# A two-layer hybrid decoder trunk on one core: direct key and value products in layer 0, its first gate's dots beside them, sums of squares by tokens in the opening, attention's turns counted from zero

## The chip, the core and the metric

The kernel runs on one core of a Trainium2 chip. The core has a matrix engine (TensorE; PE in the profile, its weight loads PEld), a vector engine (VectorE, DVE), a scalar engine (ScalarE, ACT), GpSimd (POOL) and SyncE (SP), which here only issues DMAs. The metric is the device time of one execution in microseconds, lower is better. All arithmetic is in float32; matrix products are made of float32 operands that are split in two parts, `hi` (in the format `fp32r`) and `lo` (the remainder), with three matmuls for each product: hi x hi, hi x lo and lo x hi.

## The reference, cut to what matters

Two layers over 512 tokens of 1024 channels. What the change touches is the first norm, the keys and values, and the gate `g1`:

```python
def hybrid_layer(x, c_act, ...):
    mod = (c_act @ w_ada + b_ada)[:, None, :]
    sh1, sc1, g1, sh2, sc2, g2 = jnp.split(mod, 6, axis=-1)
    h = rmsnorm(x, norm1_w) * (1 + sc1) + sh1
    u = h @ w_in
    u_pool, u_conv, b_conv, c_conv, q, k, v, gate_logits = jnp.split(u, offsets, axis=-1)
    y_pool = pool_mixer(u_pool, pool_w, pool_scale)
    y_conv = b_conv * causal_short_conv(c_conv * u_conv, conv_w)
    q = apply_partial_rope(rmsnorm(q.reshape(B, S, ATTN_HEADS, HEAD_DIM), q_norm_w), cos, sin)
    k = apply_partial_rope(rmsnorm(k.reshape(B, S, ATTN_HEADS, HEAD_DIM), k_norm_w), cos, sin)
    o = moba_attention(q, k, v)
    gates = jax.nn.sigmoid(gate_logits).reshape(B, S, N_BRANCH, D)
    merged = gates[:, :, 0] * (y_pool @ p_pool) + gates[:, :, 1] * (y_conv @ p_conv) + gates[:, :, 2] * (y_attn @ p_attn)
    x = x + g1 * (merged @ w_out)
    h2 = rmsnorm(x, norm2_w) * (1 + sc2) + sh2
    return x + g2 * ((jax.nn.silu(h2 @ w_gate) * (h2 @ w_up)) @ w_down)
```

`mod` has six parts of 1024 numbers (SH1, SC1, G1, SH2, SC2, G2 in the kernel). Each is a product of one vector with a 1024 x 1024 matrix.

## The kernel before

Activations are kept with channels on the 128 partitions and 512 tokens along the free axis, as 8 tiles. A product with a weight column is one "feature tile": 8 steps over the channels, `mm3` (L163) each, three matmuls of 512 columns.

**The stream of weights.** `items` (L374 to L389) lists the weight tiles (128 x 1024, 512 KB) in the order of use. `next_w` (L454) hands out the next one and loads up to four ahead (`load_w`, L433). A load takes one of three buffers of the ring `raw`; `split_w` (L397) then makes `hi` on ACT (L399) and `lo` on DVE (L402), each with five buffers. Some columns are split by transfer instead (`split_by_transfer`, L416): ACT makes `hi` and its negative, and a DMA of POOL's queue adds the weight to it in memory (L423). The loads are issued by SP, in order.

**Dots.** Each of the 6 x 8 pieces of `mod` of a layer is one instruction on DVE: `ada_dot` (L477, recorded as L479) multiplies a 128 x 1024 tile of `w_ada` with the conditioning vector and sums. `ada_tasks` (L530) makes a list of them with a cost of 1.2 each. With `early`, tiles come from the ring `raw`, loaded one dot ahead; without, from the pool `w4`.

**Turns.** Every `mm3` counts its columns in `clock[0]`. At 2048 columns (four products of 512) `tick` (L139) is called: it advances the fibers (attention, written as generators, which yield the number of turns to wait) and runs tasks of the queue `bulk`, as far as a credit goes that grows by `bulk_rate` for each turn, up to 4. PE's and DVE's main instructions are kept in the order of the program (`keep_in_program_order`, `pin`).

**Opening.** PE first runs idle matmuls (`WARM`, `WARM2`). x is squared on DVE and ACT (L894, L899), added in pairs on DVE (L901), and four fp32 matmuls with a matrix of ones (L902) leave the sum of squares of each token, on all partitions, as 128 x 512 numbers. ACT takes the inverse root (L908) and its scaled square (L909), two wide steps on DVE (L913, L914) refine it into `norm.rstd`, and `first_scaled` (L657) multiplies x with it. Two dots, SC1 and SH1 of tile 0, stand ahead of the refinement on DVE. Then `first_hi` (L661) makes the first operand of PE. After that, for every channel tile: two dots, scale, split of the weights, `lo`.

**Keys and values.** `keys_values` (L1001) computes the 1024 columns of keys and values with seven products of half-size blocks in place of eight (rows of tokens in two halves, channels in two halves; the names B21, B11, R1, -V, B22, T3, T4 are the forms). `sums_one` and `sums_two` (L986, L996) make the sums of activations on DVE; the class `KeyValue` (L296) loads the weights and lets DMAs of POOL's queue, DVE (L338) and `split_rows` make the sums of weights. Keys and queries are squared, normalised and rotated (`turn`, tasks of `bulk`), and values are split into `v`.

**Attention and gates.** The fiber `attention` (L858) starts five turns after the values. PE meanwhile computes gates (`gate`, L1176, tanh on ACT in L1180), convolution, and pooling branch (two products of 512 columns with `pw`, L1198). `gated` (L1209) multiplies a gate with its branch. In layer 0 the SC2 dots run here (L1202). Then come the attention branch (GATE2, L1232): a gate, a product, two steps on DVE and a split (`split_from`, L675 and L676). In this loop layer 0 runs the dots of G1 and SH2 (rate 1.5), layer 1 those of G1 (rate 1.3). The loop `tail` (L1261) makes the output projection with the residual, which needs `g1` and `merged`.

**After.** Second norm, feed-forward (also by seven products, `glu_pair`), and the next layer.

Of the kernel before, what the change touches and what calls it, by code (L numbers as in the profile page):

```python
# [73 lines left out]

WARM = 9

WARM2 = 19

GATE2 = ([("gate", j) for j in range(6)] + [("attn", 0), ("attn", 1), ("gate", 6), ("gate", 7)]
         + [("attn", j) for j in range(2, 8)])  # L80
# [3 lines left out]
def hybrid_trunk(ctx, tc, xT, ws, ada, cols, pool_w, qk_w, crow, pos, con, out):  # L84
# [69 lines left out]
    def matmul(*a, **k):  # L154
        tc.keep_in_program_order(T.matmul(*a, **k))  # L155
# [140 lines left out]
    class KeyValue:  # L296
# [25 lines left out]
        def load(self, sub):  # L322
            form, cp = divmod(sub, 2)
            if sub == 0:
                self.near, self.far = [None] * 2, [None] * 2
            if sub == 2:
                self.x = [w4([P, C_BLOCKS, P]) for _ in range(2)]
                for i in range(2):
                    self.summed(self.x[i], (1, 1), i)
            if form < 2:  # L330
                kk = 1 - form
                raw = self.raw(kk, 0, cp)
                if form == 1:
                    self.near[cp] = raw
                return split_by_transfer(raw, self.l, self.blocks(kk, 0, cp)) if self.l == 0 else split_w(raw, C_BLOCKS)
            if form in (2, 3):
                w = split_w(self.x[cp], C_BLOCKS)
                pin(V.tensor_add(self.x[cp], self.x[cp], self.near[cp]))  # L338
                if form == 2:
                    self.near[cp] = self.raw(1, 0, cp)  # L340
                    self.far[cp] = [bigt(F32) for _ in range(2)]
                    self.summed_rows(self.far[cp], (0, 0), cp)
                return w
            if form == 4:
                return split_w(self.x[cp], C_BLOCKS)
            if form == 5:
                return split_rows(self.far[cp])
            return split_w(self.raw(1, 1, cp), C_BLOCKS)
# [26 lines left out]
    for l in range(L):  # L375
        first_part = [b for b in _plan() if b[0][0] not in ("gate", "up", "down")]
        keys = [b for b in first_part if b[0][0] == "in" and KEYS <= b[0][2] < KEYS + 8]
        at_keys = first_part.index(keys[0])
        column_of = {b[0][2]: b for b in first_part if len(b) == KT and b[0][0] == "in"}
        moved = [column_of[n] for n in AFTER_KEYS]  # L380
        first_part = [b for b in first_part if b not in keys and b not in moved]
        first_part[at_keys:at_keys] = [KeyValue(l)] + moved
        for blocks in first_part + list(feed_forward()):
            if not isinstance(blocks, list):
                if isinstance(blocks, int):
                    blocks = GateUp(l, blocks)
                items += [(blocks, sub) for sub in range(blocks.SUBS)]
            else:
                items.append((None, (l, blocks)))  # L389
# [189 lines left out]


    class Norm:
        def __init__(self, one=False):
            self.one = one
            self.low = []
            self.acc = bigt(F32)
            self.last = bigt(F32)
            self.sums = [(bigt(), bigt()) for _ in range(1 if one else 2)]
            self.rstd = bigt(F32)
            self.hi = [bigt() for _ in range(KT)]
            self.lo = [bigt() for _ in range(KT)]  # L590
            self.h = [bigt(F32) for _ in range(KT)]
# [278 lines left out]


    scratch = ps_pair()
    norm = Norm()

    rows = [ps_mm(), ps_mm()]
    for i in range(WARM):
# [4 lines left out]
        if i == 6:  # L881
            for j in range(KT):
# [6 lines left out]
    pin(V.scalar_tensor_tensor(abias, colt[:, 0, C_ADA + SC1 * KT:C_ADA + (SC1 + 1) * KT], 1.0,  # L889
                               minus, op0=ALU.add, op1=ALU.mult))  # L890
    sq = [bigt(F32) for _ in range(KT)]
    for k in range(KT):
        if k == 0 or (k % 2 == 1 and k < KT - 1):
            step.append(pin(V.tensor_mul(sq[k], x[k], x[k])))  # L894
        else:
            if k in (2, 4):
                h = k // 2 - 1
                pin(A.activation(csil[:, h * S:(h + 1) * S], rows[h], AF.Copy))
            pin(A.activation(sq[k], x[k], AF.Square))  # L899
        if k % 2 == 1:  # L900
            step.append(pin(V.tensor_add(sq[k], sq[k - 1], sq[k])))  # L901
            matmul(scratch[:, 0], ones, sq[k], start=(k == 1), stop=(k == KT - 1))  # L902
    first[0].update(ada_first_load(0, step[3], (SH1,)))
    idle = ps_mm()
    for _ in range(WARM2):
        matmul(idle[:, :P], ones, ones, start=True, stop=True)
    y, y2, t = bigt(F32), bigt(F32), bigt(F32)
    A.activation(y, scratch[:, 0], AF.Abs_reciprocal_sqrt, bias=epst, scale=1.0 / D)  # L908
    split_after[0] = A.activation(y2, y, AF.Square, scale=(0.5 / D) ** 0.5)  # L909
    ada_first(0, first[0], SC1)  # L910
    ada_first(0, first[0], SH1)

    pin(V.scalar_tensor_tensor(t, scratch[:, 0], D * EPS, y2, op0=ALU.add, op1=ALU.mult))  # L913
    pin(V.scalar_tensor_tensor(norm.rstd, t, 1.5, y, op0=ALU.subtract, op1=ALU.mult))  # L914
    norm.first_scaled(0)
    norm.first_hi(0)
    fetch_after[0] = step[4]
# [19 lines left out]
    for l in range(L):  # L937
# [63 lines left out]
        def keys_values(qk, ss, made, tables, then):  # L1001
# [60 lines left out]
                V.tensor_add(part[t], part[t], d[t])  # L1062
            yield from enumerate(part)

        pw = {}

        def pool_weights():
# [58 lines left out]
        for j in range(2):  # L1126
            if j == 1:
                pu = ps_mm()
                feature_tile(pu, next_w())
                made = [sums_one(0), sums_one(1)]  # L1130
                uc[1] = bigt(F32)
                A.activation(uc[1], pu, AF.Copy)
            pc = ps_mm()
            feature_tile(pc, next_w())
            flush_bulk()
            if j == 1:
                made += [sums_one(2), sums_one(3)]
            z = bigt(F32)
            V.tensor_mul(z, pc, uc[j])
            zs.append(z)  # L1140
# [23 lines left out]
            bulk_rate[0] = 1.4  # L1164

        bulk_rate[0], credit[0] = 0.0, -1.0
        v = [[bigt().rearrange("p (n h d) -> p n h d", n=4, h=2) for _ in range(TT)] for _ in range(2)]
        for t, src in keys_values(qk, ss, made, tables, turn):
            for half in range(2):
                part = src[:, half * BLOCK:(half + 1) * BLOCK].rearrange("p (n d) -> p n d", d=HD)  # L1170
                o = v[half][t]
                A.activation(o[:, :, 0], part, AF.Copy, scale=-1.0)
                V.scalar_tensor_tensor(o[:, :, 1], part, -1.0, f32(o)[:, :, 0], op0=ALU.mult, op1=ALU.subtract)
        flush_bulk()
# [6 lines left out]
            return sg  # L1181

        m01, y_attn = [], []
        fibers.append([5, attention(l, qk, v, nrq, prq, y_attn)])
        bulk.append((0.4, pool_weights))
        for j in range(2):
# [45 lines left out]
        for step, j in GATE2:  # L1232
# [3 lines left out]
            if j == 0:  # L1236
                drain()
                flush_bulk()
                if l == 0:
                    bulk.extend(ada_tasks(l, (SH2,)))  # L1240
                late = len(bulk)
                bulk.extendleft(reversed(ada_tasks(l, (G1,))))
                bulk_rate[0] = 1.5 if l == 0 else 1.3
            if j % 2 == 0:
                aw_ = next_w()
            p1 = ps_mm()
# [324 lines left out]
```

## Time and profile before

| what | value |
|---|---|
| runs, device us | 1446.49, 1443.2, 1445.98 (median 1445.98) |
| profiled execution, from its first to its last instruction | 1440.7 us, granted clock 0.999 |
| opening, up to 16.2 us | PE busy 14.1 us, DVE 11.0, DMA share 0.90 |
| first products of layer 0, 16.2 to 71.7 | PE 55.3 of 55.5 us, DVE 48.6 |
| keys and values of layer 0, 71.7 to 110.6 | PE 38.5 of 38.9 us, DVE 36.8, ACT 29.8 |
| gates and attention of layer 0, 110.6 to 299.6 | PE 186.8 of 189.0 us, DVE 135.1 |
| attention branch of layer 0 and what follows, 299.6 to 345.0 | PE 42.9 of 45.4 us, DVE 43.4, granted clock 0.96 |
| gates and attention of layer 1, 823.8 to 1011.3 | PE 185.8 of 187.5 us, DVE 125.7 |
| attention branch of layer 1, 1011.3 to 1050.0 | PE 38.7 of 38.7 us, DVE 32.8 |

The last seven rows are from the view that gives each engine's busy time in stretches of the span. The span is what the profiler saw of one execution; the runs are 2.5 to 5.8 us longer. Matmuls are pipelined and overlap in the records, so PE's busy time hides small gaps: the starts of successive matmuls tell more.

### The profile page before, as it was taken

How to read it: one execution, taken by the hardware profiler on the slowest of the kernel's cores; microseconds unless marked ns; L12 is line 12 of the kernel's file. 1: busy time of each engine (PE TensorE's matmuls, PEld its weight loads, DVE VectorE, ACT ScalarE, POOL GpSimd, SP SyncE). 2: the span in 40 equal slices, each digit the busy share in tenths (PEclk: the TensorE clock that was granted, in tenths of full speed). 3: DMA queues.
4: the chain of work that ended last, by engine and by line, in shares of the span. 5: the costliest groups of instructions: out<-in, count | busy, mean ns of one | idle time of the engine just before them, and what ended most of it. 6: DMA issues, size and time to landing. Idle time of an engine off the chain costs nothing.

```text
span 1440.7 us, 22089 instructions
## 1 busy us (share of the span) xinstructions
PE 1428.3 (99%) x8298; PEld 1253.2 (87%) x8298; DVE 1062.3 (74%) x1944; ACT 750.8 (52%) x1260; POOL 165.7 (12%) x230
## 2 busy tenths in 40 slices
PE   9999999999999999999999999999999999999999
PEld 7887788887989998989988887888889989989997
DVE  8899767579786867767789986665878747657663
ACT  6776666633554452535454675666336525525450
POOL 0111000101100210211002000011020102111200
PEclk9999999999999999999999999999999999999999
DMA  9877666697446766747528665567773537646532
GB/s 359 234 199 192 175 162 161 159 322 236 119 128 213 196 177 203 191 131 209 195 88 248 170 149 133 133 158 186 253 207 84 141 109 180 172 109 184 138 85 85
DMA packets 94283, 251.28 MB, mean 174 GB/s; under 512 B 11992, under 2 KB 24672, under 8 KB 94176
## 3 DMA queue, kind: packets, MB, share of 16 engines
q1 hardware_dynamic: 67312, 177.37, 36.6%
q0 software_dynamic: 26272, 72.37, 25.3%
q8 instruction: 65, 1.06, 0.3%
q14 instruction: 42, 0.34, 0.1%
q10 hardware_dynamic: 592, 0.14, 0.0%
HBM read 247.73 MB, written 2.10 MB: 173 GB/s over the span
## 4 chain that ended last, share of the span: by engine, by line
PE 86%; DVE 8%; ACT 2%; DMA 2%; issue 1%; ACTq 0%; DVEq 0%; SPq 0%
PE mm L155 75%; PE pair L155 10%; DVE w L479 2%; DVE wlo L402 1%; PE mm L161 1%; DMA raw<-in_ws 1%; DMA wlo<-in_ws 0%; DVE big L676 0%; DMA w<-in_ada 0%; DVE big L1209 0%; DVE big L664 0%; DVE tmp L657 0%; ACT whi L419 0%; ACT big L675 0%; ACT whi L399 0%
## 5 line engine op out<-in xcount | busy, mean ns | idle before, releaser
L155 PE MATMUL mm<-big,whi 128*128 128x512 f32 (+1 forms) x4350 | 1080.4, 340 | 4.2 <-DVE big L676 1.9
L155 PEld LDWEIGHTS mm<-big,whi 128*128 128x128 f32 x4350 | 745.2, 190 | 92.9 <-DVE big L676 2.6
L155 PE MATMUL mm<-big,wlo 128*128 128x512 f32 (+1 forms) x2175 | 736.4, 339 | 0.4 <-DMA wlo<-in_ws 0.4
L155 PEld LDWEIGHTS mm<-big,wlo 128*128 128x128 f32 x2175 | 413.2, 190 | 46.3 <-issue 1.1
L399 ACT ACTIVATE whi<-raw 128x1024 fp32r<-128x1024 f32 (+2 forms) x186 | 191.6, 1031 | 194.1 <-PE mm L155 118.7
L402 DVE TENSOR_TENSOR wlo<-raw,whi 128x1024 fp32r<-128x1024 f32 (+2 forms) x186 | 218.8, 1185 | 41.6 <-ACT whi L399 40.9
L399 ACT ACTIVATE whi<-w 128x1024 fp32r<-128x1024 f32 x84 | 88.9, 1058 | 154.8 <-PE mm L155 94.7
L402 DVE TENSOR_TENSOR wlo<-w,whi 128x1024 fp32r<-128x1024 f32 x84 | 101.2, 1220 | 29.2 <-ACT whi L399 28.5
L1258 DVE SCALAR_TENSOR_TENSOR x<-mm,mod,x 128x512 f32<-128x512 f32 (+1 forms) x89 | 61.5, 693 | 74.1 <-PE mm L155 73.7
L479 DVE SCALAR_TENSOR_TENSOR w<-w,csil 128x1024 f32<-128x1024 f32 x88 | 105.0, 1219 | 13.0 <-DMA w<-in_ada 12.8
L261 POOL DMA_DIRECT2D w<-in_ws x72 | 47.9, 680 | 460.9 <-DVE wlo L402 258.6
L423 POOL DMA_DIRECT2D wlo<-in_ws x50 | 43.0, 861 | 388.1 <-ACT wlo L421 223.7
L263 POOL DMA_DIRECT2D w<-in_ws x72 | 63.9, 903 | 169.9 <-DMA w<-in_ws 162.8
L155 PE MATMUL pair<-whi,big 128*128 128x512 f32 x256 | 83.1, 390 | 0.0
L155 PE MATMUL pair<-big,whi 128*128 128x256 f32 (+1 forms) x376 | 74.0, 294 | 0.0
L419 ACT ACTIVATE whi<-raw 128x1024 fp32r<-128x1024 f32 x50 | 53.1, 1063 | 38.7 <-PE mm L155 28.5
L155 PEld LDWEIGHTS pair<-big,whi 128*128 128x128 f32 x376 | 60.4, 191 | 2.2
L155 PEld LDWEIGHTS pair<-whi,big 128*128 128x128 f32 x256 | 48.1, 188 | 9.9
L675 ACT ACTIVATE big<-big 128x512 fp32r<-128x512 f32 x52 | 32.5, 627 | 45.2 <-DVE big L1251 24.1
L155 PE MATMUL pair<-big,wlo 128*128 128x256 f32 (+1 forms) x188 | 55.4, 295 | 0.0
L421 ACT ACTIVATE wlo<-whi 128x1024 fp32r<-128x1024 f32 x50 | 52.6, 1059 | 0.4
L676 DVE TENSOR_TENSOR big<-tmp,big 128x512 fp32r<-128x512 f32 x48 | 33.0, 691 | 24.2 <-ACT big L675 23.2
(233 smaller groups left out, 1416.0 us busy)
## 6 DMA issues: line engine op xcount, KB each, us to landing
raw<-in_ws SPq DMA_DIRECT2D x146, 512.0 KB, 4.3
w<-in_ada SPq DMA_DIRECT2D x88, 512.0 KB, 5.8
w<-in_ws POOLq DMA_DIRECT2D x144, 256.0 KB, 4.6
wlo<-in_ws POOLq DMA_DIRECT2D x50, 512.0 KB, 6.5
raw<-in_ws SPq DMA_DIRECT2D x64, 256.0 KB, 3.8
raw<-in_ws SPq DMA_DIRECT2D x24, 384.0 KB, 3.3
raw<-in_ws SPq DMA_DIRECT2D x16, 448.0 KB, 6.4
raw<-in_ws SPq DMA_DIRECT2D x36, 128.0 KB, 3.2
```

Of the source, the lines that this page charges most:

```text
L155: tc.keep_in_program_order(T.matmul(*a, **k))
L261: nc.gpsimd.dma_start(dst, self.source(0, 1))
L263: nc.gpsimd.dma_start(dst, self.source(*other), accum_op=ALU.add)
L399: A.activation(hi[:, :n], raw[:, :n], AF.Copy)
L402: ins = V.tensor_sub(lo[:, :n], raw[:, :n], f32(hi)[:, :n])
L419: A.activation(hi[:, :n], raw[:, :n], AF.Copy)
L421: A.activation(lo[:, :n], f32(hi)[:, :n], AF.Copy, scale=-1.0)
L423: nc.gpsimd.dma_start(lo[:, i:i + m].rearrange("p b n -> p (b n)"), src, accum_op=ALU.add)
L479: return V.scalar_tensor_tensor(aw, aw, 1.0, csil, op0=ALU.mult, op1=ALU.mult, accum_out=mod[l][:, part, j:j + 1])
L675: A.activation(hi, src, AF.Copy)
L676: last_split[0] = V.tensor_sub(lo, src, f32(hi))
L1258: V.scalar_tensor_tensor(x[k][:, lo:hi], src, mod[l][:, part, k:k + 1], x[k][:, lo:hi], op0=ALU.mult, op1=ALU.add)
```

## The change

In layer 0, keys and values are computed by plain products in two stages (`keys_values_direct`): four weight tiles for the keys with four accumulators for the four token tiles, then four for the values. The weight tiles come in their old order through `split_w`; `KeyValue` serves layer 1 alone. The sums of activations are left out in layer 0, and the values are evacuated without a change of sign.

The eight dots of G1 of layer 0 are queued at the start of the keys and values, with early loads, at 1.2 a turn, and no longer in the loop of the attention branch, whose rate is 1.3 in both layers.

Ahead of attention `clock[0]` is set to 0, in both layers.

In the opening, the squared tiles become the stationary operand: for each of the four token tiles a matmul with two columns of ones leaves the sums of 128 tokens in a column. The last two squared tiles go in without being added. The inverse root and three refining steps then work on 128 x 4 numbers, and four transposes spread the result over all partitions in PSUM, where `first_scaled` reads it. The 19 idle matmuls are divided: 9 ahead of the transposes, 10 behind. The SH1 dot of tile 0 stands behind the refinement.

```diff
-WARM2 = 19
+WARM2 = (9, 10)
...
-                return split_by_transfer(raw, self.l, self.blocks(kk, 0, cp)) if self.l == 0 else split_w(raw, C_BLOCKS)
+                return split_w(raw, C_BLOCKS)
...
-        first_part[at_keys:at_keys] = [KeyValue(l)] + moved
+        first_part[at_keys:at_keys] = ([KeyValue(l)] if l else keys) + moved
...
-            self.rstd = bigt(F32)
+            self.rstd = bigt(F32) if spread else None
...
+    def sum_tokens(t, last):
+        for i in range(TT):
+            matmul(scratch[:, 0, 2 * i:2 * i + 2], t[:, i * P:(i + 1) * P], ones[:, :2],
+                   start=not groups and i == 0, stop=last, skip_group_check=True)
+        groups.append(t)
+
     for k in range(KT):
-        if k == 0 or (k % 2 == 1 and k < KT - 1):
+        if k == 0 or k % 2 == 1:
             step.append(pin(V.tensor_mul(sq[k], x[k], x[k])))
...
-        if k % 2 == 1:
+        if k >= KT - 2:
+            sum_tokens(sq[k], k == KT - 1)
+        elif k % 2 == 1:
             step.append(pin(V.tensor_add(sq[k], sq[k - 1], sq[k])))
-            matmul(scratch[:, 0], ones, sq[k], start=(k == 1), stop=(k == KT - 1))
+            sum_tokens(sq[k], False)
...
-    for _ in range(WARM2):
+    for _ in range(WARM2[0]):
         matmul(idle[:, :P], ones, ones, start=True, stop=True)
-    y, y2, t = bigt(F32), bigt(F32), bigt(F32)
-    A.activation(y, scratch[:, 0], AF.Abs_reciprocal_sqrt, bias=epst, scale=1.0 / D)
-    split_after[0] = A.activation(y2, y, AF.Square, scale=(0.5 / D) ** 0.5)
+    ss = scratch[:, 0, :2 * TT].rearrange("p (t c) -> p t c", c=2)[:, :, 0]
+    y, t, r = [sm([P, TT], tag="root", bufs=3) for _ in range(3)]
+    split_after[0] = A.activation(y, ss, AF.Abs_reciprocal_sqrt, bias=epst, scale=1.0 / D)
     ada_first(0, first[0], SC1)
+    pin(V.scalar_tensor_tensor(t, ss, D * EPS, y, op0=ALU.add, op1=ALU.mult))
+    pin(V.scalar_tensor_tensor(t, t, 0.5 / D, y, op0=ALU.mult, op1=ALU.mult))
+    pin(V.scalar_tensor_tensor(r, t, 1.5, y, op0=ALU.subtract, op1=ALU.mult))
+    for i in range(TT):
+        transpose(scratch[:, 1, i * P:(i + 1) * P], r[:, i:i + 1].to_broadcast([P, P]), ident)
+    for _ in range(WARM2[1]):
+        matmul(idle[:, :P], ones, ones, start=True, stop=True)
     ada_first(0, first[0], SH1)
-
-    pin(V.scalar_tensor_tensor(t, scratch[:, 0], D * EPS, y2, op0=ALU.add, op1=ALU.mult))
-    pin(V.scalar_tensor_tensor(norm.rstd, t, 1.5, y, op0=ALU.subtract, op1=ALU.mult))
+    norm.rstd = scratch[:, 1]
...
+        def keys_values_direct(qk, ss, tables, then):
+
+            def stage():
+                o = [ps_mm(), ps_mm()]
+                both = ps_pair()
+                o += [both[:, 0], both[:, 1]]
+                for cp in range(4):
+                    w = next_w()
+                    for t in range(TT):
+                        for i in range(2):
+                            k = 2 * cp + i
+                            mm3(o[t], cut(norm.k(k), slice(None), slice(t * P, (t + 1) * P)), wrow(w, 4 * i),
+                                k == 0, k == KT - 1)
+                return o
+
+            for t, o in enumerate(stage()):
+                qk_evac(1, qk, ss, t, o)
+            tables()
+            then()
+            yield from enumerate(stage())
...
-                made = [sums_one(0), sums_one(1)]
+                made = [sums_one(0), sums_one(1)] if l else None
...
-            if j == 1:
+            if j == 1 and l:
                 made += [sums_one(2), sums_one(3)]
...
+        if l == 0:
+            bulk.extend(ada_tasks(l, (G1,), True))
+            bulk_rate[0], credit[0] = 1.2, 0.0
...
-        for t, src in keys_values(qk, ss, made, tables, turn):
+        for t, src in (keys_values(qk, ss, made, tables, turn) if l else keys_values_direct(qk, ss, tables, turn)):
...
+                if l == 0:
+                    A.activation(o[:, :, 0], part, AF.Copy)
+                    V.tensor_sub(o[:, :, 1], part, f32(o)[:, :, 0])
+                    continue
...
+        clock[0] = 0
         fibers.append([5, attention(l, qk, v, nrq, prq, y_attn)])
...
-                bulk.extendleft(reversed(ada_tasks(l, (G1,))))
-                bulk_rate[0] = 1.5 if l == 0 else 1.3
+                if l:
+                    bulk.extendleft(reversed(ada_tasks(l, (G1,))))
+                bulk_rate[0] = 1.3
```

More of the change, by code (lines that the diff above doesn't have):

```diff
@@ L581, in hybrid_trunk, with __init__ @@
     class Norm:
-        def __init__(self, one=False):
+        def __init__(self, one=False, spread=True):
             self.one = one
@@ L872, in hybrid_trunk @@
     scratch = ps_pair()
-    norm = Norm()
+    norm = Norm(spread=False)
     rows = [ps_mm(), ps_mm()]
@@ L891, in hybrid_trunk @@
     sq = [bigt(F32) for _ in range(KT)]
+    groups = []
+    def sum_tokens(t, last):
[3 more added lines that the diff above has]
+        groups.append(t)
     for k in range(KT):
-        if k == 0 or (k % 2 == 1 and k < KT - 1):
+        if k == 0 or k % 2 == 1:
             step.append(pin(V.tensor_mul(sq[k], x[k], x[k])))
```

## The prediction

> **What bounds the kernel now.** First the page's head, its busy line and its chain of work that ended last.
>
> ```profile
> span 1440.7 us, 22089 instructions
> PE 1428.3 (99%) x8298; PEld 1253.2 (87%) x8298; DVE 1062.3 (74%) x1944; ACT 750.8 (52%) x1260; POOL 165.7 (12%) x230
> PE 86%; DVE 8%; ACT 2%; DMA 2%; issue 1%; ACTq 0%; DVEq 0%; SPq 0%
> ```
>
> TensorE sets the time: 86% of the chain is PE. So an edit counts in two ways only: matmuls more or fewer, and stalls of PE more or fewer. The price of a matmul comes from a stretch of the chain without a stall, and the stalls from the view of waits on PE.
>
> ```profile
> 83.52 5.44 PE mm L155 x24
> ```
>
> ```profile
> PE mm L155 <- DVE big L676: 1.9, 2, 1.7
> PE mm L161 <- DVE big L1209: 1.5, 1, 1.5
> ...
> PE mm L155 <- ACT big L1180: 1.0, 2, 0.5
> ```
>
> 24 matmuls of 512 columns in 5.44 us: 0.227 us each. PE waits little in all, so I took the timeline of PE around each wait and compared it with that pitch. The two layers run nearly the same program, so a stall that only one of them has is told apart by laying them side by side.
>
> **Keys and values of layer 0: direct products.** Seven forms of 2 tiles x 2 row groups x 2 x 3 = 24 matmuls are 168; direct, 2 stages x 4 weight tiles x 4 token tiles x 2 x 3 are 192. Nothing lies beside PE that could hide them: 24 x 0.227 = **+5.44 us**.
>
> What goes with the old form on other engines (the sums and differences on DVE, twelve weight sums through POOL's queue, the four tiles split by transfer) was hidden except where PE waits for a `wlo` brought by DMA:
>
> ```profile
> 79.77 0.62 PE L155 MATMUL pair<-whi,big 128*128 128x512 f32 x2
> 80.77 0.47 PE L155 MATMUL pair<-wlo,big 128*128 128x512 f32 x1 [0.38 <-DMA wlo<-in_ws]
> ```
>
> ```profile
> 115.99 0.61 PE L155 MATMUL mm<-big,whi 128*128 128x512 f32 x2
> 116.98 0.47 PE L155 MATMUL mm<-big,wlo 128*128 128x512 f32 x1 [0.37 <-DMA wlo<-in_ws]
> ```
>
> Two matmuls should take 0.45 us and took 1.00 and 0.99: 0.55 us lost at each place. In the old form a weight tile serves 12 matmuls (2.7 us), so four tiles of lookahead are 10.9 us; direct, a tile serves 24 (5.44 us), and the lookahead is 21.8 us. Both waits should go: **-1.1 us** (bounds -1.1 and 0).
>
> **The first gate's dots, moved.** Before, the sixteen dots of G1 and SH2 run beside the attention branch of layer 0, and PE then stalls where the output projection begins:
>
> ```profile
> 337.11 0.39 PE L155 MATMUL mm<-big,whi 128*128 128x512 f32 x1
> 339.18 0.50 PE L155 MATMUL mm<-big,whi 128*128 128x512 f32 x1 [1.68 <-DVE big L676]
> ...
> 340.52 0.50 PE L155 MATMUL mm<-big,whi 128*128 128x512 f32 x1 [0.61 <-ACT big L675]
> 341.25 0.79 PE L155 MATMUL mm<-big,whi 128*128 128x512 f32 x1 [0.23 <-DVE big L676]
> ...
> 344.36 0.39 PE L155 MATMUL mm<-big,wlo 128*128 128x512 f32 x1
> ```
>
> Eleven matmuls start from the first of these rows up to the last: 2.49 us at the usual pitch, 7.25 us here, so 4.76 us are lost. A part is the clock, from the view of stretches (its columns: stretch, length, busy time of PE, PEld, DVE, ACT, POOL, granted clock, DMA share, GB/s):
>
> ```profile
> 337.40:340.85 3.45, 1.17 (x4) 0.48 (x3) 2.75 (x6) 0.99 (x2) 0.00 (x0) 1.00 0.61 178
> 340.95:344.25 3.30, 3.07 (x8) 2.43 (x8) 3.30 (x4) 2.08 (x3) 0.00 (x0) 0.50 0.59 189
> ```
>
> After 3.45 us with PE busy for 1.17, the next 3.3 us run at half clock. Layer 1 is the test of what eight dots do in this place; the same view, of the dots' line L479 alone:
>
> ```profile
> 299.60:338.60 39.00, 19.04 (x32) 1.00 0.84 311
> 1011.30:1050.00 38.70, 9.48 (x16) 1.00 0.62 229
> ```
>
> Layer 0 spends 19.0 us of DVE on sixteen dots (two records each), layer 1 9.5 us on eight, and layer 1 shows no wait of PE there. After the change layer 0 has eight, the SH2 ones, at layer 1's rate of 1.3. I take the whole stall off: **-4.76 us** (bounds -4.76 and 0). Next in line behind it is DVE again, with 9.5 us less to do in 39.
>
> The eight dots reappear in the key and value stretch, one for each turn of 2.7 us. Their loads, 512 KB each, go onto SP's queue between the weight loads and into the weights' ring of three buffers, so a dot in DVE's order can wait for its DMA with the next `wlo` queued behind it. I cost that at nothing; what covers it is the lookahead of 21.8 us, priced below as a rival.
>
> **Turns counted from zero.** In layer 0 the counter stands at zero there anyway (136 products of 512 columns before it, 144 after the change: both multiples of four). In layer 1 it stands at 1024, from the two pooled products of layer 0, so the edit moves layer 1's turns by two products, into layer 0's positions. What that is worth is seen where eight transposes are followed by a gate's matmul, layer 0 first:
>
> ```profile
> 166.94 1.04 PE L161 MATMUL mm<-ident,tmp 128*128 128x128 f32 x8
> 167.74 0.70 PE L155 MATMUL mm<-big,whi 128*128 128x512 f32 x2
> ```
>
> ```profile
> 869.96 0.74 PE L155 MATMUL mm<-big,whi 128*128 128x512 f32 x2 [0.58 <-DVE big L1209]
> ```
>
> ```profile
> 876.72 1.04 PE L161 MATMUL mm<-ident,tmp 128*128 128x128 f32 x8
> 878.26 0.73 PE L155 MATMUL mm<-big,whi 128*128 128x512 f32 x2 [0.50 <-ACT big L1180]
> ```
>
> ```profile
> 918.18 1.04 PE L161 MATMUL mm<-ident,tmp 128*128 128x128 f32 x8
> 919.72 0.73 PE L155 MATMUL mm<-big,whi 128*128 128x512 f32 x2 [0.50 <-ACT big L1180]
> ```
>
> From the transposes to the gate's matmul it is 0.80 us in layer 0 and 1.54 twice in layer 1: 0.74 lost each time, and 0.58 at 869.96. **-2.06 us** (bounds -2.6, with smaller gaps, and +2 if the turns land as badly elsewhere). Layer 0's own stall at 159 us (1.5 us behind L1209) follows a burst of SC2 dots whose place and order stay; I keep it.
>
> **The opening.** Rows in order of time, PE's weight loads first:
>
> ```profile
> 4.49 1.73 PEld L161 LDWEIGHTS mm<-ident,ccol 128*128 128x128 f32 x8
> 4.55 0.17 DVE L889 SCALAR_TENSOR_TENSOR abias<-colt,minus 128x8 f32<-128x8 f32 x1
> ...
> 9.50 0.30 PEld L155 LDWEIGHTS pair<-big,ones 128*128 128x128 f32 x2 [1.10 <-DVE big L901]
> ...
> 10.34 1.23 DVE L479 SCALAR_TENSOR_TENSOR w<-w,csil 128x1024 f32<-128x1024 f32 x1
> ...
> 11.42 4.41 PE L155 MATMUL mm<-ones 128*128 128x128 f32 x38
> ...
> 11.69 0.69 ACT L908 ACTIVATE big<-pair,epst 128x512 f32<-128x512 f32 x1 [2.01 <-PE pair L155]
> ...
> 13.80 0.69 DVE L914 SCALAR_TENSOR_TENSOR big<-big,big 128x512 f32<-128x512 f32 x1
> 14.61 0.75 DVE L657 SCALAR_TENSOR_TENSOR tmp<-x,am,big 128x512 f32<-128x512 f32 x1
> ```
>
> Removed: four wide steps from 11.69 to 14.49. Added: one small ACT step and three small DVE steps (0.17 us each, 0.2 apart: some 0.8 us), four transposes, and sums by tokens that cost eight weight loads a tile. Here lies the choice. Two loads of fp32 data in 0.30 us, one being 0.19, are 0.11 apart; loads for transposes are closer:
>
> ```profile
> 124.57 0.14 PEld L161 LDWEIGHTS mm<-ident,w 128*128 128x128 f32 x1
> ```
>
> ```profile
> 159.92 0.20 PEld L161 LDWEIGHTS mm<-ident,tmp 128*128 128x128 f32 x2 [0.39 <-ACT tmp L809]
> ```
>
> (0.20 less 0.14: 0.06). The last three groups are 24 loads from 9.50 on. At 0.11 they end at 12.1; nine idle matmuls of two records at 0.112 (4.41 us for 38) hold PE's queue until 14.1, the transposes 0.6 longer, and L657 starts at 14.75, against 14.61. At 0.06 it starts near 13.6. Behind the transposes on PE stand ten more idle matmuls and the first products; behind L657 on DVE the first `wlo`. I take 0.11, the row of the same kind of load: **+0.15 us** (bounds -1.0 and +0.15). The Trainium skill ("TensorE: Matmul & The Clock Gate", section on LDWEIGHTS) gives a load as its columns over 1.2 ns, 107 ns for 128. By that the sum is the same; the transposes' closer row speaks against it as a rule for all loads.
>
> **Sum.** 5.44 - 1.1 - 4.76 - 2.06 + 0.15 = -2.33 us: a span of 1438.4 for 1440.7. The three runs have a median of 1445.98, 5.3 above the span; carrying the difference over gives 1443.6. About 0.3%, 4.3 us, is what a measurement of this kernel can tell from no change, so this is within it.
>
> **Rivals.**
> - *Opening faster* (chance 0.20): loads at 0.06. For it: that row. Against: the loads of `big`. 1.15 less: 1442.5.
> - *The stall at 159 goes too* (0.08): DVE has less left over from the key stretch. Against: the burst of dots stays as it was. Some 2 less: 1441.6.
> - *Clock gate in the opening* (0.12), slower than before. With two columns a matmul the array is nearly idle from 9.5 to 12, as it was ahead of the half clock at 340.95. If loads don't count as work, clock and loads halve: the row at 4.49 has half-clock loads 0.21 apart, so 24 cost 5.1 for 2.6, the idle matmuls 4.0 for 2.0, the transposes 0.8 for 0.4: +4.9 and 1448.5. It decides from about two thirds of a 3.4 us window idle (1.17 of 3.45 busy above). The Trainium skill (same page, Part 1 on the clock gate) says that a free-running window of some 3.4 us sends an idle array to half clock; the trace agrees (3.3 us at 0.50), and the page doesn't say whether a weight load counts.
> - *Turns don't help layer 1* (0.08): 2.06 more, 1445.7: that part then doesn't do what it is there for.
> - *The ring of three* (0.06), slower too. Rows of the page and of the chain:
>
> ```profile
> L402 DVE TENSOR_TENSOR wlo<-w,whi 128x1024 fp32r<-128x1024 f32 x84 | 101.2, 1220 | 29.2 <-ACT whi L399 28.5
> raw<-in_ws SPq DMA_DIRECT2D x146, 512.0 KB, 4.3
> ```
>
> ```profile
> 73.61 7.02 DMA wlo<-in_ws
> ```
>
> A weight tile with its two dots takes landing + split (about 2.3) + dot 1.2 + issue 0.3 in turn: 8.1 us at 4.3, against PE's 5.44. Four such tiles fall 10.7 us behind, and 21.8 less 6.6 are there. It decides from a landing of about 5.2 us; at 7.0, 9 us are lost: 1452.6.
> - *As forecast* (0.46): 1443.6, give or take 1.3, the spread of the runs.
>
> Range: 1440.6 to 1447.8. It leaves out the ring, half of the clock's case and the edges, under 0.2. Faster by over 0.3% (below 1441.6) takes half of the case of 159 us, a third of the fast opening and the low edge of the forecast with gaps as wide as their bounds: 0.25. Slower by over 0.3% (above 1450.3) is the ring and the top of the clock's case: 0.08. Within: 0.67.
>
> **What would show it.** Right: 192 matmuls at 0.227 in the key stretch with no wait for `wlo`; no wait behind L676 and no half clock near 340 us; 0.80 us from transposes to gate in layer 1; L657 between 13.6 and 14.8 us. Wrong: half clock before 20 us; DVE waiting for `in_ada` between 75 and 100 us and PE for a `wlo` soon after; a stall that DVE causes in layer 0 past 300 us; new waits for L1180 or L1209 in layer 1.

## The result: slower by half a per cent, and the profile after

The changed kernel takes 1452.23 us (median of 5 runs, 1449.51 to 1453.42), the kernel before 1445.81 beside it (5 runs, 1442.07 to 1446.49). The ratio is 1.0053, with a 95% interval of 1.0038 to 1.0068: slower. The medians lie 6.4 us apart; the ratio, by which the runs are compared from here on, stands for 7.7. The forecast was 1443.6, the range ended at 1447.8: both were wrong.

The page of the changed kernel, its head and its chain:

```profile
span 1451.7 us, 22099 instructions
PE 1436.6 (99%) x8358; PEld 1266.5 (87%) x8358; DVE 1040.9 (72%) x1905; ACT 734.0 (51%) x1234; POOL 152.3 (10%) x214
PE 90%; DMA 4%; DVE 3%; issue 2%; ACT 1%; SPq 0%; POOL 0%; DVEq 0%; ACTq 0%; POOLq 0%
```

DVE, ACT and POOL have less to do than before, and the span is 11.0 us longer (1451.7 for 1440.7). A shorter busy time of the other engines says nothing, then; the waits on PE say more:

```profile
PE pair L155 <- DVE tmp L657: 6.4, 1, 6.4
PE mm L161 <- DVE big L1253: 1.4, 1, 1.4
PE pair L155 <- POOL ones L207: 1.1, 1, 1.1
PE mm L155 <- DVE wlo L402: 0.8, 1, 0.8
```

The first row is new: a single wait of 6.4 us for the scaled step of the first norm. The others are old (L1253 is the branch step that was L1209) or small. The stall behind L676 and the waits for L1180 are gone. To see where the loss is complete, compare the first matmul of the keys and values, in the timeline of PE, before and after:

```profile
71.77 0.39 PE L155 MATMUL pair<-whi,big 128*128 128x512 f32 x1
```

```profile
85.73 0.39 PE L155 MATMUL mm<-whi,big 128*128 128x512 f32 x1
```

13.96 us are lost ahead of this point. Of what was changed in the keys, the dots and the turns, little lies ahead of it, VectorE's sums of activations above all, and they are left out. So the loss must lie in the opening (e1 and e2 below test that), and the other parts must have gained. The timeline of PE in the opening of the changed kernel (start, length, engine, line, operation, count, the wait before it):

```profile
6.69 1.05 PE L155 MATMUL pair<-ones,big 128*128 128x2 f32 x8
8.47 6.68 PE L155 MATMUL pair<-ones,big 128*128 128x2 f32 x32 [0.73 <-DVE big L911]
15.01 4.19 PE L155 MATMUL mm<-ones 128*128 128x128 f32 x18
18.99 0.69 PE L161 MATMUL pair<-ident,root 128*128 128x128 f32 x4
...
21.67 0.47 PE L155 MATMUL mm<-whi,big 128*128 128x512 f32 x1
...
23.77 0.40 PE L155 MATMUL pair<-whi,big 128*128 128x512 f32 x1
30.58 0.79 PE L155 MATMUL pair<-whi,big 128*128 128x512 f32 x1 [6.42 <-DVE tmp L657]
```

and the view of stretches (columns as in the prediction: PE, PEld, DVE, ACT, POOL, granted clock, DMA share, GB/s):

```profile
5.60:8.90 3.30, 2.57 (x23) 2.42 (x21) 2.87 (x5) 2.30 (x5) 0.00 (x0) 1.00 1.02 370
8.95:19.10 10.15, 10.15 (x49) 10.14 (x49) 4.23 (x10) 2.21 (x5) 0.00 (x0) 0.50 1.03 414
19.20:29.40 10.20, 4.96 (x33) 3.98 (x32) 9.02 (x13) 4.84 (x9) 0.00 (x0) 1.00 0.71 257
29.45:36.20 6.75, 5.62 (x13) 4.45 (x14) 6.75 (x12) 4.48 (x9) 0.00 (x0) 0.50 0.90 298
```

The first product of the kernel before, in the same view:

```profile
16.23 0.51 PE L155 MATMUL mm<-whi,big 128*128 128x512 f32 x1 [0.40 <-ACT big L661]
```

Read together: the 32 sums take 0.209 us each on average (6.68 for 32, the first few still at full clock) where 0.11 was forecast, because the clock is at half from about 9 to 19 us. "PE busy 10.15 of 10.15" hides it: the records show the queue as full, and only the clock column and the pitch show that it is slow. The first product starts at 21.67, 5.44 us later than before. Then comes the wait of 6.4 us; from 23.77 to 30.58, less one pitch, it costs 6.6. Behind it comes a second stretch at half clock, in which 13 matmuls (30.58 to 36.2) take 0.427 for 0.227 us: about 2.6 us more. 5.44 + 6.6 + 2.6 is 14.6; the remaining 0.7 is given back in small gaps between the first matmuls, which the kernel before had (its third waits until 17.08).

Behind the opening the terms of the sum can be checked. The stretch around the start of the output projection (now near 355 us), and the dots' line L479 in the 39 us ahead:

```profile
353.00:358.00 5.00, 5.00 (x24) 4.14 (x23) 5.00 (x7) 2.70 (x4) 0.00 (x0) 1.00 0.32 106
```

```profile
314.00:353.00 39.00, 9.49 (x16) 1.00 0.72 261
```

PE's records follow each other without a wait, at full clock, and the dots take 9.5 us as in layer 1. Layer 1's turns, transposes and the gate's matmul behind them:

```profile
891.09 1.04 PE L161 MATMUL mm<-ident,tmp 128*128 128x128 f32 x8
891.88 0.70 PE L155 MATMUL mm<-big,whi 128*128 128x512 f32 x2
...
931.79 1.03 PE L161 MATMUL mm<-ident,tmp 128*128 128x128 f32 x8
932.58 0.70 PE L155 MATMUL mm<-big,whi 128*128 128x512 f32 x2
```

0.79 us from one to the other, for 1.54 before, at both places. New and small are two waits where weights are late, the first just behind layer 0's output projection, the second at the start of layer 1's gates:

```profile
414.58 0.50 PE L155 MATMUL mm<-big,wlo 128*128 128x512 f32 x1 [0.77 <-DVE wlo L402]
...
843.94 0.47 PE L155 MATMUL mm<-big,wlo 128*128 128x512 f32 x1 [0.34 <-DMA wlo<-in_ws]
```

### The profile page after: what moved, and what is told of

Read it like the earlier page. It is cut to its first block, busy times and chain, and to the rows that moved or that the text cites. A ratio compares the mean times of both kernels' runs of the same rounds, so it can differ in the third digit from the quotient of the medians.

```text
span 1451.7 us, 22099 instructions
## 1 busy us (share of the span) xinstructions
PE 1436.6 (99%) x8358; PEld 1266.5 (87%) x8358; DVE 1040.9 (72%) x1905; ACT 734.0 (51%) x1234; POOL 152.3 (10%) x214
## 3 DMA queue, kind: packets, MB, share of 16 engines
q1 hardware_dynamic: 67312, 177.37, 36.2%
## 4 chain that ended last, share of the span: by engine, by line
PE 90%; DMA 4%; DVE 3%; issue 2%; ACT 1%; SPq 0%; POOL 0%; DVEq 0%; ACTq 0%; POOLq 0%
PE mm L155 78%; PE pair L155 10%; PE mm L161 1%; DMA raw<-in_ws 1%; DVE raw L479 1%; DMA raw<-in_ada 1%; DMA wlo<-in_ws 1%; DMA tmp<-in_pool_w 1%; DVE wlo L402 0%; DMA x<-in_xT 0%; ACT whi L399 0%; DVE w L479 0%; ACT whi L419 0%; DVE big L1151 0%; DVE tmp L657 0%
## 5 line engine op out<-in xcount | busy, mean ns | idle before, releaser
L399 ACT ACTIVATE whi<-raw 128x1024 fp32r<-128x1024 f32 (+2 forms) x192 | 198.1, 1032 | 225.6 <-PE mm L155 132.6
L402 DVE TENSOR_TENSOR wlo<-raw,whi 128x1024 fp32r<-128x1024 f32 (+2 forms) x192 | 226.0, 1186 | 54.0 <-ACT whi L399 53.4
L399 ACT ACTIVATE whi<-w 128x1024 fp32r<-128x1024 f32 x78 | 82.5, 1058 | 150.5 <-PE mm L155 89.1
L402 DVE TENSOR_TENSOR wlo<-w,whi 128x1024 fp32r<-128x1024 f32 x78 | 94.0, 1221 | 30.4 <-ACT whi L399 29.7
L479 DVE SCALAR_TENSOR_TENSOR w<-w,csil 128x1024 f32<-128x1024 f32 x80 | 95.3, 1220 | 15.1 <-DMA w<-in_ada 15.1
L423 POOL DMA_DIRECT2D wlo<-in_ws x46 | 39.3, 855 | 469.5 <-ACT wlo L421 221.2
L155 PE MATMUL pair<-whi,big 128*128 128x512 f32 x240 | 79.7, 392 | 6.4 <-DVE tmp L657 6.4
L419 ACT ACTIVATE whi<-raw 128x1024 fp32r<-128x1024 f32 x46 | 49.0, 1065 | 24.7 <-PE mm L155 14.5
L421 ACT ACTIVATE wlo<-whi 128x1024 fp32r<-128x1024 f32 x46 | 48.5, 1057 | 0.5
L676 DVE TENSOR_TENSOR big<-tmp,big 128x512 fp32r<-128x512 f32 x48 | 33.0, 691 | 21.5 <-ACT big L675 20.5
L155 PE MATMUL pair<-wlo,big 128*128 128x512 f32 x120 | 47.0, 392 | 0.0
```

What stands on the lines that cost most here:

```text
L399: A.activation(hi[:, :n], raw[:, :n], AF.Copy)
L402: ins = V.tensor_sub(lo[:, :n], raw[:, :n], f32(hi)[:, :n])
L419: A.activation(hi[:, :n], raw[:, :n], AF.Copy)
L421: A.activation(lo[:, :n], f32(hi)[:, :n], AF.Copy, scale=-1.0)
L423: nc.gpsimd.dma_start(lo[:, i:i + m].rearrange("p b n -> p (b n)"), src, accum_op=ALU.add)
L479: return V.scalar_tensor_tensor(aw, aw, 1.0, csil, op0=ALU.mult, op1=ALU.mult, accum_out=mod[l][:, part, j:j + 1])
```

## The experiments

Theory A: the opening alone loses the 14 us, by two causes. Sums that stream two columns leave the array idle, so the clock gate closes; and the products' fourth accumulator lies in the same pair of PSUM banks (`pair_a, pair_b = ps_pair(), scratch`, and `pair_b[:, 0]` as the last of `q_ps`) as the spread roots, `norm.rstd = scratch[:, 1]`, so that PE's first write there is ordered behind VectorE's reads of the other half (three scaled steps stand ahead of it in the program). Rivals: the loss lies in the key stretch; VectorE is simply late; the loads or the gaps, not the columns, close the gate.

| run | ratio to before, 95% interval | median, us (before beside it) |
|---|---|---|
| the changed kernel | 1.0053 [1.0038, 1.0068] | 1452.23 (1445.81) |
| e1: with the old opening | 0.9964 [0.9951, 0.9976] | 1439.72 (1444.07) |
| e2: before, with the new opening | 1.0072 [1.0050, 1.0093] | 1455.13 (1444.07) |
| e3: roots copied to SBUF | 1.0002 [0.9989, 1.0016] | 1444.39 (1444.07) |
| e4: sums of 128 columns | 1.0027 [1.0015, 1.0039] | 1447.89 (1444.07) |
| e5: both | 0.9965 [0.9953, 0.9978] | 1440.02 (1444.53) |
| e7: e1 without the reset of the turns | 0.9980 [0.9971, 0.9989] | 1441.42 (1444.53) |
| e9: before, with direct products alone | 1.0011 [1.0001, 1.0022] | 1446.48 (1444.53) |
| e10: before, with dots and turns alone | 1.0042 [1.0029, 1.0055] | 1451.13 (1444.53) |
| e11: e5 with the idle matmuls divided 5, 14 | 0.9971 [0.9961, 0.9982] | 1440.01 (1444.08) |
| e12, e13: e5 with sums of 32, 64 columns | one run each | 1443.91, 1439.54 (1444.08) |

Each row without another number has 4 to 12 runs. Below, a difference of 0.0010 in the ratio is 1.44 us.

**e1, the old opening.**

```diff
-WARM2 = (9, 10)
+WARM2 = 19
...
-            sum_tokens(sq[k], False)
+            matmul(scratch[:, 0], ones, sq[k], start=(k == 1), stop=(k == KT - 1))
...
-    norm.rstd = scratch[:, 1]
+    pin(V.scalar_tensor_tensor(t, scratch[:, 0], D * EPS, y2, op0=ALU.add, op1=ALU.mult))
+    pin(V.scalar_tensor_tensor(norm.rstd, t, 1.5, y, op0=ALU.subtract, op1=ALU.mult))
```

> The changed kernel with the opening of the kernel before (sums of squares by ones as the stationary tile, the wide steps of the norm, 19 idle matmuls). Theory: the opening alone loses the 14.0 us that lie between the two traces at the start of the keys and values (85.73 for 71.77 us), and the other parts are worth what they were sized at: 1452.2 - 14.0 = 1438.3 us, faster than the kernel before by some 7 us, no half clock before 40 us. Rival: the loss comes from the first gate's dots in the key stretch or the direct products as well, and the opening only shows it first: then this kernel stays near 1446 to 1452.

0.9964: faster than before, with an interval that lies wholly below 1. Its clock, in the stretch up to 36 us:

```profile
2.00:36.00 34.00, 31.48 (x149) 24.14 (x149) 28.76 (x46) 20.23 (x37) 0.00 (x0) 1.00 0.98 358
```

No half clock. Its keys start here:

```profile
72.93 0.39 PE L155 MATMUL mm<-whi,big 128*128 128x512 f32 x1
```

That is 12.80 us ahead of the changed kernel (85.73), and from 1.0053 to 0.9964 are 12.9 us for the opening: theory A's place is right, and the other parts together gain. With the same opening these keys start 1.16 us later than before (71.77): by so much two traces can differ.

**e2, the new opening alone.** The same edit the other way round, on the kernel before.

> The kernel before with nothing but the new opening. Theory: slower than before by the same 14.0 us: 1459.8 us, with half clock from about 9 to 19 us and again from about 29 to 36, and TensorE waiting some 6.4 us behind the third scaled step of the norm (L657). Rival: the pooled products of layer 0 absorb part of it, because there are waits for weights there at 80 and 116 us that a late start covers: then 1458.7 or less.

```profile
30.34 0.80 PE L155 MATMUL pair<-whi,big 128*128 128x512 f32 x1 [6.44 <-DVE tmp L657]
```

```profile
85.51 0.39 PE L155 MATMUL pair<-whi,big 128*128 128x512 f32 x1
```

The wait comes with the opening, and so does the late start of the keys: 13.74 us behind the row of before. In the ratio it is 10.4 us (7.2 to 13.4). That is less than the 13.7 of the two traces: the profiled run of before (1443.2 us) was quicker than its median, and from 80 us on, where weights were late, the two traces come closer, as the rival said: by 0.9 us up to the matmul that starts at 119.35 before and at 132.23 here.

**e3, the roots copied.**

```diff
-    norm = Norm(spread=False)
+    norm = Norm()
...
-    norm.rstd = scratch[:, 1]
+    A.activation(norm.rstd, scratch[:, 1], AF.Copy)
```

> The changed kernel, with the transposed roots copied by ScalarE from PSUM into SBUF, so that VectorE's scaled steps no longer read the pair of PSUM banks that the products want to write. Theory: TensorE's wait of 6.4 us behind the third scaled step goes, because it came from the shared pair of banks and not from the data; the second stretch of half clock (29 to 36 us) goes with it, some 8 us less in all and about 0.7 us more for the copy: 1444 to 1445 us, with the first half clock still there. Rival: VectorE is simply late with the third tile and the products want its result at that point: the wait stays under another name, 1452 to 1453 us.

1.0002 for 1.0053: 7.4 us. The wait of 6.4 us isn't in its waits any more, although a copy was added and VectorE has as much to do: products ran on at once. The second matmul of the row at 21.21 is the first into the fourth accumulator, and the third scaled step (L657) starts at 27.23, so the products had not wanted the third scaled tile:

```profile
21.21 0.62 PE L155 MATMUL pair<-whi,big 128*128 128x512 f32 x2
```

```profile
27.23 0.75 DVE L657 SCALAR_TENSOR_TENSOR tmp<-x,am,big 128x512 f32<-128x512 f32 x1
```

The half clock behind the wait is gone too. The first half clock is still there, in the profiled run for one stretch of some 3.4 us, when the sums are all but over:

```profile
12.00:15.40 3.40, 3.40 (x17) 3.40 (x17) 1.63 (x5) 1.48 (x3) 0.00 (x0) 0.50 1.02 413
```

In the changed kernel it was about 10.2 us long, three times that, with the same sums. The Trainium skill ("TensorE: Matmul & The Clock Gate", Part 1) says that the gate watches a free-running window of 3413 ns, so that a kernel's number of slow matmuls differs from run to run; the trace agrees, with stretches of about 3.4, 6.8 and 10.2 us here. e3's own runs differ in this way too: in three of the ten, the profiled one among them, the mean granted clock is 0.998, in the other seven 0.996. One stretch of 3.4 us at half takes 0.0012 off the mean clock of such a run, so by this estimate the seven hold some two stretches more; they take 1444.27 to 1446.14 us, the three 1441.49 to 1443.37. So the ratio tells what the copy is worth, and this one trace shows the first half clock shorter than most runs of e3 have it. That slow sums last longer, and so fill more windows, is likely but not shown.

**e4, sums of 128 columns.**

```diff
-            matmul(scratch[:, 0, 2 * i:2 * i + 2], t[:, i * P:(i + 1) * P], ones[:, :2],
+            matmul(scratch[:, 0, i * P:(i + 1) * P], t[:, i * P:(i + 1) * P], ones,
...
-    ss = scratch[:, 0, :2 * TT].rearrange("p (t c) -> p t c", c=2)[:, :, 0]
+    ss = scratch[:, 0].rearrange("p (t c) -> p t c", c=P)[:, :, 0]
```

> The changed kernel, with all 128 columns of ones streamed in the sums by tokens, where two columns were streamed. The loads stay as many as they were. Theory (the array counts as idle when a matmul streams two columns, and the clock gate closes on it): full clock up to the start of the products, sums 0.11 us apart, first scaled step at 14.7 us for 19.8; the wait of 6.4 us behind the third scaled step stays, since that has nothing to do with the clock: about 1447 us. Rival: it is the gaps between the groups of sums that close the gate, or the loads themselves take 0.21 us: half clock as before, 1452 us or more.

```profile
5.60:19.00 13.40, 13.09 (x101) 12.16 (x100) 10.71 (x19) 6.92 (x13) 0.00 (x0) 1.00 1.03 407
...
25.90:30.30 4.40, 4.40 (x10) 3.47 (x11) 4.40 (x7) 2.86 (x5) 0.00 (x0) 0.50 0.94 331
```

```profile
25.89 0.80 PE L155 MATMUL pair<-whi,big 128*128 128x512 f32 x1 [6.43 <-DVE tmp L657]
```

As many loads, 64 times the columns, and it is faster: full clock up to 19 us. So it was neither the loads nor the gaps that closed the gate. The wait behind L657 stays at 6.4 us, and half clock follows it again, for 4.4 us here. 1.0027 for 1.0053 is 3.8 us; 5.2 had been expected, which the two intervals leave possible.

**e5, both mends.**

> The changed kernel with both mends of the opening at once: the sums stream all 128 columns, and the transposed roots are copied into SBUF. Theory (two separate causes, clock gate and shared PSUM pair, that add up to the loss): no half clock before 40 us, no wait behind the scaled steps, the first scaled step near 15.8 us (0.7 for the copy) and the first product near 17.7 us for 16.2 before: some 1.5 us slower than with the old opening, so 1441 us, 3 us faster than the kernel before. Rival (the copy alone already took all that matters, because PE has slack behind the opening): the same as with the copy alone, 1444 us.

The clock up to 40 us, and the first product:

```profile
5.00:40.00 35.00, 34.60 (x192) 29.50 (x191) 31.53 (x51) 20.02 (x37) 0.00 (x0) 1.00 0.97 359
```

```profile
17.16 0.50 PE L155 MATMUL mm<-whi,big 128*128 128x512 f32 x1
```

Neither the half clock nor the wait is left. 0.9965, 12.7 us below the changed kernel, where the mends give 7.4 and 3.8 alone. They are separate causes that add up; the rest is within the intervals.

**e12 and e13, 32 and 64 columns**, to see from where the gate closes, with the copied roots.

> The changed kernel with the copied roots, and with 32 columns streamed in each matmul of the sums. A load takes 0.11 us, 32 columns are a quarter of what 128 take in the same time, so the array is idle for some three quarters of the stretch from 8 to 12 us. If the gate goes by the idle share of a window of about 3.4 us (it closed after a window with 1.17 busy of 3.45, a third): half clock for at least one window between 9 and 16 us. Rival: any stream of some length between loads keeps it open: full clock.

> The same with 64 columns: the array is busy for about half of the stretch, above the third at which the gate was seen to close: full clock throughout, first product near 17.2 us as with 128 columns. Rival: the gate wants more than half of the window busy: half clock for at least one window between 9 and 16 us, first product near 18.9 us as with two columns and the copy.

The same stretch, first with 32 columns, then with 64:

```profile
11.00:14.40 3.40, 3.40 (x17) 3.40 (x17) 1.01 (x2) 0.24 (x2) 0.00 (x0) 0.50 1.02 412
```

```profile
11.00:14.40 3.40, 3.40 (x32) 3.40 (x32) 2.01 (x6) 1.40 (x3) 0.00 (x0) 1.00 1.03 411
```

If 128 columns of this format stream for 0.11 us, the pitch of the idle matmuls, which is also that of the loads, then by this estimate the array streams for about a quarter of the time with 32 columns, and the clock is at half; with 64 for about half of it, and the clock is full. With one run each, it is likely but not shown that the limit lies between the two. PE's busy column, 3.40 in both, can't tell them apart.

**e9, direct products alone**, on the kernel before (the diff's parts for `KeyValue`, `keys_values_direct`, the sums and the values; dots, turns and opening as before).

> The kernel before with nothing but the direct products for the keys and values of layer 0. Theory: 24 more matmuls (+5.44 us) and two waits for weights gone (-1.1), while the stall near 337 us and layer 1's turns stay as they were: 4.3 us slower than before, ratio 1.0030. Rival: with 12 weight sums and the sums on VectorE gone, VectorE is early for the stall at 337 us, which then shrinks without the move of the dots: no slower than before.

+1.6 us (0.1 to 3.2): slower, so the theory has the sign, but 4.3 lies outside the interval. The stall at the output projection is there. By the prediction's way of counting it is 4.6 us (eleven matmuls in 7.08 us from 341.14 to 348.22, less 2.49) for 4.76, with almost as many dots ahead (17.9 us of them):

```profile
341.14 0.40 PE L155 MATMUL mm<-big,whi 128*128 128x512 f32 x1
343.46 0.50 PE L155 MATMUL mm<-big,whi 128*128 128x512 f32 x1 [1.92 <-DVE big L676]
...
348.22 0.63 PE L155 MATMUL mm<-big,wlo 128*128 128x512 f32 x1
```

```profile
302.00:341.00 39.00, 17.91 (x30) 1.00 0.90 326
```

So the rival (a stall that shrinks by itself) is wrong. Why the cost is 2.7 us less than forecast is settled in part only. In the traces the first matmul of the keys starts at 71.77 before and at 72.44 here, and the same matmul just ahead of the stall at 336.21 and at 339.70: up to there the direct products cost 2.8 us, not 4.3, so besides the two waits that the prediction counted PE lost some 1.5 us less. The rest stays open. The runs of before beside it lie between 1441.21 and 1448.04, so a typical run of it may hold waits that its profiled one doesn't show; and e9's profiled run, 1450.61, is the longest of its twelve, with a wait of 2.87 us for a `wlo` brought by DMA at 836.78.

**e7, without the reset of the turns.**

```diff
-        clock[0] = 0
```

> The changed kernel with the old opening and without the reset of the turn counter. Theory: the counter moves only layer 1's turns, and TensorE waits there again behind L1208 and its neighbours, 1.54 us from transposes to gate for 0.80: 2.1 us slower than with the reset by the three places counted in the prediction, up to 3.5 by the offsets of the two traces, so 1442 to 1443 us. Rival: the gain in layer 1's attention comes from VectorE having less to do, not from the turns: no difference, 1439.7 us.

0.9980 for 0.9964 with the reset: 2.3 us, though the two intervals overlap a little. The trace shows the delay back where the prediction had counted it:

```profile
875.96 1.04 PE L161 MATMUL mm<-ident,tmp 128*128 128x128 f32 x8
877.49 0.73 PE L155 MATMUL mm<-big,whi 128*128 128x512 f32 x2 [0.50 <-ACT big L1208]
```

And from e9 to e7, which differ in the dots alone, it is 0.0031, 4.5 us: the stall at the output projection.

**e10, the dots and the turns without direct products.** On the kernel before:

```diff
+        if l == 0:
+            bulk.extend(ada_tasks(l, (G1,), True))
+            bulk_rate[0], credit[0] = 1.2, 0.0
...
+        clock[0] = 0
...
-                bulk.extendleft(reversed(ada_tasks(l, (G1,))))
-                bulk_rate[0] = 1.5 if l == 0 else 1.3
+                if l:
+                    bulk.extendleft(reversed(ada_tasks(l, (G1,))))
+                bulk_rate[0] = 1.3
```

> The kernel before with the first gate's dots beside the keys and values and the turn counter reset, but with the pooled products of layer 0 and the old opening kept. Theory 1 (the dots fit there without the direct products): the stall at 337 us goes (-4.8) and layer 1's turns gain 2.1 to 3.5, with no 24 matmuls more: 7 to 8 us faster than before, ratio 0.995, and 3 us faster than the changed kernel with the old opening. Theory 2 (the direct products are what makes room for the dots): beside pooled products VectorE and the weight ring, with 10.9 us of lookahead, cannot take eight dots in 35 us; TensorE waits there for weights, some 5 to 9 us, and the kernel is no faster than before.

1.0042, slower: theory 2. Two waits of PE in the keys and values, and pieces of the chain ahead of them, two landings of the ring's loads and the `wlo` that ends the second wait:

```profile
93.60 0.50 PE L155 MATMUL pair<-wlo,big 128*128 128x512 f32 x1 [4.68 <-DVE wlo L402]
...
126.95 0.79 PE L155 MATMUL mm<-big,wlo 128*128 128x512 f32 x1 [8.44 <-DVE wlo L402]
```

```profile
84.73 6.41 DMA raw<-in_ada
...
112.51 5.60 DMA raw<-in_ws
...
125.76 1.14 DVE wlo L402
```

The two waits are 13.1 us. The prediction's rival of the ring of three buffers has its part in them, beside pooled products and not beside direct ones. But it isn't all: between the landing that ends at 118.11 and the `wlo` at 125.76 the chain holds, beside the making of `hi` on ACT, some 6 us of VectorE's own steps. The direct products are what makes room for the dots. Whether they do it by the longer lookahead or by what they take off VectorE and the DMA queues, no run separates.

**e11, fewer idle matmuls ahead of the transposes**: `WARM2 = (5, 14)` in e5.

> The kernel with both mends of the opening, with 5 idle matmuls ahead of the transposes and 14 behind for 9 and 10. Theory: the roots are ready on VectorE at 13.43 us while idle matmuls hold TensorE's queue until 14.33; with four calls (eight records of 0.11) less the transposes start 0.85 us earlier, and so does all that follows: 1439.2 us, ratio 0.9959. Rival: VectorE's dot that stands ahead of the first scaled step ends at 14.6 us in any case, so of the 0.85 only what lies between 14.6 and the copy's end counts, and with noise nothing is seen: the ratio of 0.9965 again.

0.9971, no gain. The edit brought its own wait. Idle matmuls of PE and the first product behind them:

```profile
14.54 3.29 PE L155 MATMUL mm<-ones 128*128 128x128 f32 x28
17.59 0.48 PE L155 MATMUL mm<-whi,big 128*128 128x512 f32 x1
```

The 28 records behind the transposes last until 17.6, so the first product, which came at 17.16 in e5 with 20 of them, waits for idle work: its operand is ready at 16.94, when L661 ends on ACT. The fastest versions are e1 and e5, 0.9964 and 0.9965: about 5 us faster than before. Mended, the new opening is worth nothing that can be measured against the old one.

## Why the prediction was wrong, step by step

- **The opening: this step failed.** The prediction said "I take 0.11, the row of the same kind of load: +0.15 us (bounds -1.0 and +0.15)". It was +13.96 in the traces and 12.9 in the ratios (e1). Two things were behind it. First, the rival of the clock gate was true: the sums took 0.209 us each, and the first scaled step came at 19.81 for 14.75. Its price of 4.9 us was fair (first product 5.44 late), its chance of 0.12 was low, and its cost was missing from the bounds of the step. Its own condition, an array idle for two thirds of a window, was met by two columns beside loads of 0.11 us, if loads don't count as work; the prediction left that open, and e4, e12 and e13 show loads that don't keep the clock up. One reading was weaker than it looked: the prediction calls the loads at 4.49 half-clock ones by their pitch of 0.21 us, while the clock column gives 1.00 there; the price held all the same. Second, the wait of the next point.
- **The wait that wasn't on the list: the opening's second failure.** Some 9 us of the 14 come from the wait behind L657 and the half clock that it causes (7.4 by e3's ratio). The diff shows it: `norm.rstd` moves from a tile of its own in SBUF to one half of a pair of PSUM banks whose other half is the products' fourth accumulator. The prediction asked what the transposes cost, and not who else writes where their result now lives.
- **Keys and values, +5.44 and -1.1:** the matmuls (192 in 43.5 us) and the two waits came as forecast in the trace; by e9's ratio the whole is +1.6 (0.1 to 3.2), so the term was mis-sized by some 2.7 us. "Nothing lies beside PE that could hide them" was too strong: in e9's trace 1.5 of the 2.7 are won back ahead of the output projection. The cause of the rest is open.
- **The dots, -4.76:** right in place and size, 4.5 by e9 and e7; no half clock and no wait near 355 us. Nothing in the keys waited for the dots there, as the prediction expected of the lookahead of 21.8 us; e10 shows the price beside pooled products. The price of 9 us that the prediction gave its rival of the ring doesn't come out of its own terms: at a landing of 7.0 us four tiles of 10.8 against 5.44 fall 21.4 behind, and 21.8 less 6.6 leave 6.2 lost.
- **The turns, -2.06:** right, 2.3 by e7 and e1, 0.79 us from transposes to gate.
- **The stall at 159 us stays:** right. It is the row of waits for L1253, 1.4 us.

Without the opening's term the sum was -2.48; the measured one is -5.2 (-7.1 to -3.5, e1). The difference is the size of what the keys' term was off by.

## What to carry to other kernels

When a result moves to another memory, list everyone who writes or reads the tile that it moves into, other parts of that tile too: the order is kept here for the pair as a whole, and three readers of one half held up a writer of the other for 6.4 us. Price an edit to TensorE's idle or start-up work at both clocks, and judge it by columns streamed per load, not by the busy column. A form with more matmuls on the engine that is the bound can pay when it leaves its feeders room: the direct products, 24 matmuls longer (1.6 us by e9's ratio), took in dots whose removal from a later place was worth 4.5; beside the shorter form the same move brought 13 us of waits.

## What the runs showed of the hardware

- Matmuls of 2 or 32 columns behind loads of 128 columns let the granted clock fall to 0.50; with 64 and 128 columns, and as many loads, it stays at 1.00 (32 and 64: one run each).
- At half clock a load with its sum takes some 0.21 us for 0.11 and a matmul of 512 columns 0.427 for 0.227. The Trainium skill ("TensorE: Matmul & The Clock Gate", Part 1) gives the start-to-start time of a cold array as N over 1.2 GHz, 426.7 ns for 512 columns; the trace agrees.
- A stall of 6.4 us on PE cost about 2.6 us more behind it in the changed kernel, as 13 matmuls at half clock; in e4 the half clock behind the same stall lasted 4.4 us for 6.75.
